# Second attention of a two-layer diffusion backbone: another spread of two projections, and orders between products

## The chip, the cores and the metric

The kernel runs on one core of one Trainium2 chip. The metric is the device time of one execution in microseconds (us). In the profile the engines are called PE (TensorE matmul), PEld (TensorE weight load), DVE (VectorE), ACT (ScalarE), POOL (GpSimd) and SP (SyncE, which issues most of the DMAs here). A name like L465 is a line of the kernel.

## What is computed

The model has two layers over 1024 latent tokens and 256 context tokens with 1024 features. The first layer has a global and a windowed attention side by side. The second layer has a convolution module and a two-dimensional neighbourhood attention side by side; the results of both go through one output projection. The change lies in the second layer's attention. Cut to that, the reference is:

```python
cv, cgl, cg, dq, dk, dv, dg = split_cols(h_lat @ w_in, ODD_WIDTHS)
c_dk, c_dv = heads(x_dk, 8), heads(x_dv, 8)          # context keys and values
oc = conformer_conv(cv, cgl, cg, dw_w, dw_b, ln_g, ln_b)
def d_row(args):                                     # one grid row of 64 queries
    r, qr = args
    rs = clip(r - 4, 0, rows - 8)                    # 8 rows of keys around it
    kk = concat([c_dk, k_grid[rs : rs + 8]])
    vv = concat([c_dv, v_grid[rs : rs + 8]])
    return gqa_attend(qr, kk, vv, bias)              # softmax(q k / 8 + bias) v
od = lax.map(d_row, (arange(rows), q_rows))
y_lat = concat([oc, od * silu(dg)]) @ w_out
return rms_norm(x_lat + g_l * y_lat, final_g)
```

## The kernel before

**Number format.** Each float32 operand of a product is split into a high and a low part. A product is then three matmuls that accumulate into one bank: high by high, high by low, low by high (`mm3`, lines L318, L320, L319). `split` (L296 for the high part, L299 for the low part) makes the two parts. The last matmul of the latest product is kept in `done[0]`.

**Projections of the second attention.** The eight heads are worked in four pairs. `d_proj(i)` projects query, key, value and gate of pair `i`: 31 steps, each a yield after two or three of the eight 128-feature slices `dk`. The order is query chunk 1, query chunk 2, key chunks 1, 2 and 0 (the context), and then, with new weights, value and gate of chunks 1 and 2 and the value of chunk 0. One chunk has 512 tokens, the context 256. A chunk's eight slices are 24 matmuls. The results go to DRAM (`QD`, `KD`, `VD`, `GD`) and are loaded from there. Weights come through `load_w` (L329 loads, eight buffers each for the high and low part, so that the eight slices of one half take all of them). Pairs 0 and 1 are projected beside the convolution and the layer norm. The layer norm (`ln_steps`, L1157 to L1164) uses a memory pool that is closed before the pool of the attention opens; the keys (`KAt`, loaded at L361) are among the tiles that come into that space.

**Attention.** `attn_gen` walks over 16 groups (one head, half of the query columns each) with 7 tiles of keys: 112 tiles. It is a generator: twelve steps of start-up (maxima `mx`, L1342 and L1350, of the first two groups), then two steps a tile. The first step of a tile emits its score product (`st`, L465 and L469), the addition of the bias, the exponential and the split; the second emits the value product (`ov`, L409 to L411) of the tile three before. The first matmul of each score product is appended to the list `sts`, which is shared by both layers.

**Order.** `weave(main, nmain, fill, nfill, ...)` takes `nmain` steps of the attention and spreads `nfill` steps of a projection among them. The fill steps get a priority that is 98 instructions earlier (`FL`), and a planner orders the instructions of each engine by priority and its own estimate of when they are ready. With `lag` above zero a fill step's TensorE instructions are put behind the score product that is `lag` from the end of `sts` (`tc.issue_after`, an order on the engine and no semaphore). Each engine works through its queue in the planned order.

The second attention weaves like this: 73 steps with `d_proj(2)` (31 fill steps), 53 with `d_proj(3)` (31), 77 with the first half of the output projection `out1_part(range(4))` (32), 24 with further parts of it (8), and 12 with its end. The output projection's first half reads the convolution's result (`oc`, loaded and split by `out1_alloc` into buffers that held the normalized tokens).

Of the kernel before, what the change touches and what calls it, by code (L numbers as in the profile page):

```python
# [53 lines left out]
PCB = 3  # L54
MODP = ((), (1, 3, 6))
FL = (80, -98)
LAG = (0, 0, 6, 12)
WV = (73, 53, 77, 24, 12)
SQ = (0, 1)
EV0 = "e0 c0 f0".split()  # L60
EVS = "e1 c1 e2 f1 c2 f2".split()
# [5 lines left out]
ENDS = ((0, 0, 512), (1, 0, 256), (1, 256, 256))  # L67
LATE = 100
NFILL = (34, 34, 34)
HV = (('gggvvvvg',) * 3, ('gggvvvvg', 'vvvgvvvg', 'gggvvvvg'))  # L70
O1 = (6, 84, 46, 14)
TICK0, TICK1 = (1, 3)
# [15 lines left out]
def tile_kernel(ctx: ExitStack, tc: tile.TileContext, a, out):  # L88
    nc = tc.nc
    VE, SC, GP, PE, SY = nc.vector, nc.scalar, nc.gpsimd, nc.tensor, nc.sync  # L90
# [8 lines left out]
    turn = [0, 0]  # L99
    mk, mwp, hold, layer = [0], [None], [0], [0]  # L100
    sts, pvs = [], []

    def bank(tag, name):
        if tag == "pp" and solo[0]:
            turn[0] += 1
            tag = ("pp", "mx")[turn[0] // 2 % 2]
        return ps.tile([P, 512], F32, tag=tag, name=name, bufs=BUFS[tag])
# [3 lines left out]
    def nm(s):  # L111
        uid[0] += 1
        return f"{s}_{uid[0]}"
# [150 lines left out]
    @contextmanager  # L264
    def later(n):

        p = tc.cur_priority
        tc.cur_priority = p + n
        yield
        tc.cur_priority -= n  # L270
# [23 lines left out]
    def split(src, hi, lo, heng="s", leng="g"):  # L294
        if heng == "s":
            SC.copy(hi, src)  # L296
        else:
            VE.tensor_copy(hi, src)
        (GP if leng == "g" else VE).tensor_tensor(lo, src, hi.bitcast(F32), op=ALU.subtract)  # L299

    def make_h(l, c, xs, bc, h):

        cond = 1 if c == 0 else 0
        for dk in range(DK):
            x = xs(dk)
            VE.scalar_tensor_tensor(x, x, gs[l][:, dk, cond : cond + 1], bc, op0=ALU.mult, op1=ALU.mult)
            shift = modT[l][:, dk, cond : cond + 1]
            if HV[l][c][dk] == "v":
                SC.activation(h[0][:, dk, :], x, AF.Identity, bias=shift)
# [2 lines left out]
                SC.activation(x, x, AF.Identity, bias=shift)  # L312
                split(x, h[0][:, dk, :], h[1][:, dk, :])

    done = [None]

    def mm3(o, lh, ll, rh, rl, first, last):
        PE.matmul(o, lh, rh, start=first, stop=False)  # L318
# [73 lines left out]
    def attn_gen(pool, groups, vshare, look, nexts=None):  # L392
# [43 lines left out]
        def prepare(x, n):  # L436

            while n and work and work[0][0] <= x:
                if next(work[0][1], work) is work:
                    work.pop(0)  # L440
                else:
                    n -= 1
# [7 lines left out]
        for x, (g, t) in enumerate(items):  # L450
            if x + AHEAD < len(items):
                items[x + AHEAD][0].ahead(items[x + AHEAD][1])
            if t == 0:
                g.start()
                while any(p is g.prep for _, p in work):
                    prepare(len(items), 1)
                for k in g.ids:
                    next(preps[k])
                    work.append((x + LEAD[layer[0]], preps[k]))
            rate = g.rate * max(len(work), 1)  # L460
            k, q0, n, extra = g.tiles[t]
            KA, KB = g.k()
            st = bank("st", nm("st"))
            cs = slice(k * P, (k + 1) * P)
            sts.append(PE.matmul(st[:, :n], KA[:, cs], g.QH[:, q0 : q0 + n], start=True, stop=False))  # L465
            if not g.bias:
                for lhs, rhs in extra():
                    PE.matmul(st[:, :n], lhs, rhs, start=False, stop=False)
            PE.matmul(st[:, :n], KB[0:68, cs], g.QL[0:68, q0 : q0 + n], start=False, stop=True)  # L469
            ph = pool.tile([P, 512], F32R, tag="ph", name=nm("ph"), bufs=look + 1)  # L470
            pl = pool.tile([P, 512], F32R, tag="pl", name=nm("pl"), bufs=look + 1)
            pf = pool.tile([P, 512], F32, tag="pf" if layer[0] else "ost", name=nm("pf"), bufs=PFB)
            if g.bias and extra is not None:
                VE.tensor_tensor(pf[:, :n], st[:, :n], extra(), op=ALU.add)
                SC.activation(pf[:, :n], pf[:, :n], AF.Exp)
            else:
                SC.activation(pf[:, :n], st[:, :n], AF.Exp, scale=1.0 if g.bias else SCALE)  # L477
            cnt[0] += 1
            split(pf[:, :n], ph[:, :n], pl[:, :n], "s", "v" if cnt[0] % vshare == 0 else "g")
            pend.append((g, t, ph, pl))  # L480
            if t == len(g.tiles) // 2:
                g.gate()
            if t == len(g.tiles) - 1:
                g.last()
            prepare(x, rate // 2)
            yield
            if len(pend) > look:
                flush()
            prepare(x, rate - rate // 2)
            yield  # L490
# [1 line left out]
            flush()  # L492
            yield

    def weave(main, nmain, fill, nfill, last=True, all_fill=True, lag=0):

        done = 0
        for k in range(nmain):
            next(main, None)
            while done * nmain < (k + 1) * nfill:  # L500
                with ExitStack() as cx:
                    cx.enter_context(later(FL[layer[0]]))
                    if lag and len(sts) >= lag:
                        cx.enter_context(tc.issue_after(sts[-lag].ins))
                    next(fill, None)
                done += 1
        if all_fill:
            for _ in fill:
                pass
        if last:  # L510
            for _ in main:
                pass
# [139 lines left out]
    with ExitStack() as p0x:  # L652
# [229 lines left out]
        main = attn_gen(a0, [group0(u, qb) for u in ORDER for qb in QORD], VS0, LOOK0)  # L882
        for k in range(3):
            u = ORDER[k]
            n = NSTEP[u // 2] + (12 if k == 0 else 0)
            n0 = 0 if k else N0
            if not k:
                weave(main, n0, proj_gate(u, gblocks(k)[1]), 9, False)
            weave(main, n - n0 - NLAST[u // 2], fill0(k + 1), NFILL[k], False)
            weave(main, NLAST[u // 2], proj_gate(ORDER[k + 1], gblocks(k + 1)[1]), 18, False)  # L890
# [208 lines left out]
    with ExitStack():  # L1099
# [337 lines left out]
        def out1_part(fs, ks=(0, 1)):  # L1437
            for e2 in range(4):
                w = load_w(wp, a["od_wo"], e2 * 256, 256, 256, WB, dks=fs)
                for e in (2 * e2, 2 * e2 + 1):  # L1440
                    if fs[0] == 0:
                        x2_load(e)
                    for k in ks:
                        yield from out1(fs, e, k, *w)
# [57 lines left out]
                    yield from final_norm(k, bcs[k])  # L1502

        main = attn_gen(dpool, groups1, VSH, LOOK1, {11: [], 12: [13, 14], 13: [15]})
        weave(main, WV[0], d_proj(2), 31, False, True, LAG[0])
        weave(main, WV[1], d_proj(3), 31, False, True, LAG[1])
        run(out1_alloc())
        weave(main, WV[2], out1_part(range(4)), 32, False, True, LAG[2])
        assert fin[0] >= 12
        for hf in (1, 0):  # L1510
            od_load(hf)
        weave(main, WV[3], out1_part((4, 5, 6), (1,)), 8, False, True, LAG[3])
        assert fin[0] >= 14
        weave(main, WV[4], ends(EV0), NEV, False, True)
        wend = [load_w(wp, a["od_wo"], e2 * 256, 256, 256, WB, lambda dk: "gv"[dk % 2], dks=[7]) for e2 in range(4)]
# [118 lines left out]
```

## Time and profile before

| | us |
|---|---|
| median of 3 runs | 1556.66 |
| range of the runs | 1556.37 to 1558.11 |
| profiled execution | 1555.72 |
| span of the profiled execution | 1553.9 |
| TensorE busy in the span | 1449.1 |
| mean granted TensorE clock | 0.967 |

In the tables of the trace by stretches each row has the stretch, its length, and for each engine its busy time and, in brackets, its instructions; then the mean granted TensorE clock (1 is full), the DMA engines' busy share and the GB/s moved. In a timeline a row has start, duration, engine, line, operation, output and inputs, and in square brackets the idle time before it with what ended it. Matmuls are pipelined, so a duration of 0.40 us for a 512-column matmul is longer than the distance to the next.

### The profile page before, as it was taken

What the parts mean: (1) busy time and instruction counts of PE and PEld (TensorE: products, weight loads), DVE (VectorE), ACT (ScalarE), POOL (GpSimd) and SP (SyncE); (2) the same over time, 40 slices, a digit from 0 to 9 for tenths busy, and PEclk for the clock granted to TensorE, in tenths of its full rate; (3) what the DMA queues carried; (4) which work ended last, traced back from release to release, by engine and by line L of the source; (5) the groups of instructions that cost most, each with busy time, mean ns of one, the idle gap of its engine ahead of it and who ended that gap; (6) DMA issues with size and microseconds to landing.
All of it is one profiled execution on the core that took longest, in us unless ns stands there. A gap on an engine that the chain in (4) does not pass through costs nothing.

```text
span 1553.9 us, 22052 instructions
## 1 busy us (share of the span) xinstructions
PE 1449.1 (93%) x6984; PEld 1172.3 (75%) x6984; DVE 1123.3 (72%) x2172; ACT 759.8 (49%) x1545; POOL 833.5 (54%) x762
## 2 busy tenths in 40 slices
PE   6989989999999989899999889999999999799995
PEld 1878868887789678678887668888787787687784
DVE  4998898689858666654577677999755457586776
ACT  2721354445454755565455555443434455545563
POOL 1561464555555676675455666664542443545574
PEclk9999999999999999999999999999999999899996
DMA  9548245423441124631111121213456888788623
GB/s 339 194 146 270 79 125 174 147 64 121 151 129 44 54 89 143 207 115 56 42 45 35 68 95 57 80 63 123 158 178 222 272 225 263 221 264 240 192 92 109
DMA packets 185614, 221.01 MB, mean 142 GB/s; under 512 B 17421, under 2 KB 139481, under 8 KB 185497
## 3 DMA queue, kind: packets, MB, share of 16 engines
q1 hardware_dynamic: 178832, 208.03, 43.1%
q10 hardware_dynamic: 6664, 11.57, 2.3%
q8 instruction: 55, 0.90, 0.2%
q14 instruction: 63, 0.51, 0.1%
HBM read 159.51 MB, written 60.03 MB: 141 GB/s over the span
## 4 chain that ended last, share of the span: by engine, by line
PE 67%; DVE 12%; DMA 11%; issue 3%; POOL 3%; ACT 2%; SPq 2%; DVEq 0%; ACTq 0%; POOLq 0%
PE p L320 6%; PE p L318 6%; PE p L319 6%; PE ov L409 4%; PE ov L410 4%; PE ov L411 4%; PE st L465 4%; PE po L318 4%; PE st L469 4%; PE po L319 4%; PE po L320 4%; PE pq L320 2%; PE pq L319 2%; PE pq L318 2%; DMA mw<-in_mod_w_dram 2%
## 5 line engine op out<-in xcount | busy, mean ns | idle before, releaser
L299 POOL TENSOR_TENSOR pl<-pf,ph 128x512 fp32r<-128x512 f32 (+4 forms) x321 | 399.9, 1258 | 270.7 <-ACT ph L296 218.9
L299 POOL TENSOR_TENSOR wl<-wr,wh 128x256 fp32r<-128x256 f32 (+2 forms) x256 | 197.7, 788 | 227.9 <-ACT wh L296 203.3
L477 ACT ACTIVATE pf<-st 128x512 f32<-128x512 f32 x284 | 166.2, 596 | 161.7 <-PE st L469 106.3
L296 ACT CAST ph<-pf 128x512 fp32r<-128x512 f32 (+4 forms) x364 | 209.2, 588 | 25.5 <-PE ov L410 17.6
L296 ACT CAST wh<-wr 128x256 fp32r<-128x256 f32 (+2 forms) x264 | 103.2, 404 | 172.2 <-DMA wr<-in_od_d_dram 39.3
L318 PE MATMUL p<-hh,wh 128*128 128x512 f32 x448 | 177.7, 399 | 3.7 <-DVE spk L299 1.4
L319 PE MATMUL p<-hl,wh 128*128 128x512 f32 x448 | 177.9, 398 | 0.2 <-POOL hl L299 0.2
L320 PE MATMUL p<-hh,wl 128*128 128x512 f32 x448 | 175.2, 399 | 0.1
L465 PE MATMUL st<-QH,KAt 128*128 128x512 f32 (+4 forms) x364 | 144.0, 397 | 19.8 <-ACT pf L477 16.5
L409 PE MATMUL ov<-ph,Vt 128*128 128x512 f32 (+4 forms) x364 | 143.6, 394 | 8.8 <-DVE y L631 6.4
L411 PE MATMUL ov<-pl,Vt 128*128 128x512 f32 (+4 forms) x364 | 143.7, 395 | 3.9 <-POOL pl L299 3.8
L410 PE MATMUL ov<-ph,Vt 128*64 128x512 f32 (+4 forms) x364 | 140.8, 387 | 0.0
L469 PE MATMUL st<-QL,KBt 68*128 68x512 f32 (+4 forms) x364 | 138.2, 388 | 0.8 <-DVE QL L388 0.7
L1116 DVE SCALAR_TENSOR_TENSOR cps<-U,taps,cps 128x512 f32<-128x512 f32 x184 | 124.3, 747 | 0.0
L589 DVE TENSOR_REDUCE mp<-mx 128x1 f32<-128x512 f32 x128 | 85.5, 682 | 33.5 <-PE mx L588 32.7
L219 DVE SCALAR_TENSOR_TENSOR macc<-mw,csil,macc 128x512 f32<-128x512 f32 x107 | 97.5, 929 | 14.0 <-DMA mw<-in_mod_w_dram 13.2
L318 PEld LDWEIGHTS p<-hh,wh 128*128 128x128 f32 x448 | 84.6, 189 | 24.5 <-DVE spk L299 1.6
L465 PEld LDWEIGHTS st<-QH,KAt 128*128 128x128 f32 x364 | 69.8, 192 | 42.5 <-ACT pf L477 25.3
L319 PEld LDWEIGHTS p<-hl,wh 128*128 128x128 f32 x448 | 84.6, 189 | 20.4 <-POOL hl L299 0.6
L320 PEld LDWEIGHTS p<-hh,wl 128*128 128x128 f32 x448 | 84.6, 189 | 20.3 <-POOL wl L299 1.0
L411 PEld LDWEIGHTS ov<-pl,Vt 128*128 128x128 f32 x364 | 71.1, 195 | 28.1 <-POOL pl L299 7.6
L409 PEld LDWEIGHTS ov<-ph,Vt 128*128 128x128 f32 x364 | 71.5, 196 | 24.3 <-issue 7.0
(277 smaller groups left out, 3518.4 us busy)
## 6 DMA issues: line engine op xcount, KB each, us to landing
mw<-in_mod_w_dram SPq DMA_DIRECT2D x34, 512.0 KB, 5.6
bs<-in_d_bs_dram SPq DMA_DIRECT2D x16, 832.0 KB, 7.3
Q<-qs SPq DMA_DIRECT2D x40, 256.0 KB, 2.7
QH<-Q SPq DMA_DIRECT2D x80, 128.0 KB, 2.7
bm<-in_d_bm_dram SPq DMA_DIRECT2D x16, 540.0 KB, 6.1
wr<-in_od_d_dram SPq DMA_DIRECT2D x64, 128.0 KB, 2.6
mw<-in_mod_w_dram SPq DMA_DIRECT2D x28, 256.0 KB, 3.1
wr<-in_ev_qkv_dram SPq DMA_DIRECT2D x32, 192.0 KB, 3.8
```

Source lines behind the costliest of these rows:

```text
L296: SC.copy(hi, src)
L299: (GP if leng == "g" else VE).tensor_tensor(lo, src, hi.bitcast(F32), op=ALU.subtract)
L318: PE.matmul(o, lh, rh, start=first, stop=False)
L319: PE.matmul(o, lh, rl, start=False, stop=False)
L320: done[0] = PE.matmul(o, ll, rh, start=False, stop=last)
L409: PE.matmul(o, V[:, 64:192], ph[:, :n], start=(t == 0), stop=False)
L410: PE.matmul(g.ov[0:64, q0 : q0 + n], V[:, 0:64], ph[:, :n], start=False, stop=False)
L411: pvs.append(PE.matmul(o, V[:, 64:192], pl[:, :n], start=False, stop=(last and g.sink is None)))
L465: sts.append(PE.matmul(st[:, :n], KA[:, cs], g.QH[:, q0 : q0 + n], start=True, stop=False))
L469: PE.matmul(st[:, :n], KB[0:68, cs], g.QL[0:68, q0 : q0 + n], start=False, stop=True)
L477: SC.activation(pf[:, :n], st[:, :n], AF.Exp, scale=1.0 if g.bias else SCALE)
L1116: VE.scalar_tensor_tensor(pc, uc, w, pc, op0=ALU.mult, op1=ALU.add)
```

## The change

`d_proj(3)` is spread over 73 attention steps instead of 53, and the first half of the output projection over 57 instead of 77 (the sum of the first three weaves stays 203). `LAG` becomes 4 in the first three weaves, where it was 0, 0 and 6. A new number `TIE = 2` puts the score product of an attention step behind the last matmul of the last but one fill step of the same weave. For that, `weave` keeps a list `past` of the last matmul after each fill step, and `attn_gen` reads `tied[0]`. (`prods` is the same list as `done` in the outer function; it has another name because `weave` has a local `done`.)

```diff
-LAG = (0, 0, 6, 12)
-WV = (73, 53, 77, 24, 12)
+LAG = (4, 4, 4, 12)
+WV = (73, 73, 57, 24, 12)
+TIE = 2
...
+    tied = [None]
...
-    done = [None]
+    done = prods = [None]
...
-            sts.append(PE.matmul(st[:, :n], KA[:, cs], g.QH[:, q0 : q0 + n], start=True, stop=False))
+            with ExitStack() as cx:
+                if tied[0] is not None:
+                    cx.enter_context(tc.issue_after(tied[0].ins))
+                sts.append(PE.matmul(st[:, :n], KA[:, cs], g.QH[:, q0 : q0 + n], start=True, stop=False))
...
-    def weave(main, nmain, fill, nfill, last=True, all_fill=True, lag=0):
+    def weave(main, nmain, fill, nfill, last=True, all_fill=True, lag=0, tie=0):
 
         done = 0
+        past = []
         for k in range(nmain):
+            tied[0] = past[-tie] if tie and len(past) >= tie else None
             next(main, None)
+            tied[0] = None
             while done * nmain < (k + 1) * nfill:
                 with ExitStack() as cx:
                     cx.enter_context(later(FL[layer[0]]))
                     if lag and len(sts) >= lag:
                         cx.enter_context(tc.issue_after(sts[-lag].ins))
                     next(fill, None)
+                past.append(prods[0])
                 done += 1
...
-        weave(main, WV[0], d_proj(2), 31, False, True, LAG[0])
-        weave(main, WV[1], d_proj(3), 31, False, True, LAG[1])
+        weave(main, WV[0], d_proj(2), 31, False, True, LAG[0], TIE)
+        weave(main, WV[1], d_proj(3), 31, False, True, LAG[1], TIE)
         run(out1_alloc())
-        weave(main, WV[2], out1_part(range(4)), 32, False, True, LAG[2])
+        weave(main, WV[2], out1_part(range(4)), 32, False, True, LAG[2], TIE)
```

## The prediction

> **What bounds the kernel now.** I read the page first, then the busy time of each engine by stretches of the second attention, then TensorE's timeline at the borders of those stretches, and last what TensorE waited for. The page says that TensorE is the engine to watch:
>
> ```profile
> span 1553.9 us, 22052 instructions
> PE 1449.1 (93%) x6984; PEld 1172.3 (75%) x6984; DVE 1123.3 (72%) x2172; ACT 759.8 (49%) x1545; POOL 833.5 (54%) x762
> ```
>
> The span is 1553.9 us. Inside the part that the change touches I cut at events: the first product of the third head pair (1172.7), its 63rd (1189.2), the first key load landed (1212.7), the last product of the fourth pair (1334.5), the first output product (1361.6), a key wait (1446.6), the last scores (1518).
>
> ```profile
> core 0: us, PE busy (x) PEld busy (x) DVE busy (x) ACT busy (x) POOL busy (x), PEclk, DMA share, GB/s
> 1172.70:1189.20 16.50, 16.47 (x80) 13.63 (x81) 10.34 (x22) 6.12 (x14) 5.00 (x6) 1.00 0.70 224
> 1189.20:1212.70 23.50, 20.19 (x97) 16.09 (x95) 6.99 (x14) 7.60 (x16) 9.27 (x12) 1.00 0.74 223
> 1212.70:1230.40 17.70, 17.10 (x81) 13.50 (x82) 9.10 (x24) 5.21 (x10) 0.00 (x0) 1.00 1.06 327
> 1230.40:1334.50 104.10, 99.11 (x516) 81.75 (x515) 70.87 (x170) 57.35 (x128) 46.03 (x51) 0.98 0.79 239
> 1334.50:1361.60 27.10, 19.59 (x78) 14.66 (x79) 14.10 (x35) 14.84 (x31) 12.76 (x14) 0.75 0.89 232
> 1361.60:1446.60 85.00, 80.39 (x393) 65.07 (x391) 63.31 (x155) 44.60 (x91) 42.18 (x44) 1.00 0.88 251
> 1446.60:1518.00 71.40, 70.94 (x337) 57.97 (x338) 50.94 (x106) 45.38 (x100) 50.00 (x52) 0.98 0.40 122
> ```
>
> Stretch minus PE busy is idle: 0.0 + 3.3 + 0.6 + 5.0 + 7.5 + 4.6 + 0.5 = 21.5 us. One minus PEclk, times the stretch, is what the slower clock took: 2.1 (fourth pair's stretch) + 6.8 (27.1 x 0.25) + 1.4 = 10.3 us. No product is added or removed, so the change can only move this loss of 31.8 us. Its worst part is 1334.5 to 1361.6: 7.5 + 6.8 = 14.3 us in which attention runs without a projection beside it.
>
> Why that hole is there:
>
> ```profile
> 1315.63 1.89 DVE L299 TENSOR_TENSOR oc<-oc 128x512 fp32r<-128x512 f32 x3
> 1337.42 1.67 POOL L299 TENSOR_TENSOR wl<-wr,wh 128x256 fp32r<-128x256 f32 x2
> 1361.22 0.50 PE L465 MATMUL st<-QH,KAt 128*128 128x512 f32 x1
> 1361.78 0.40 PE L318 MATMUL po<-oc,wh 128*128 128x512 f32 x1
> ```
>
> The inputs of the output projection were split by 1317.5 and its first weights by about 1339, yet its first product comes at 1361.78, right behind a score product. The score count by stretch says which one:
>
> ```profile
> core 0: us, PE busy (x) PEld busy (x), PEclk, DMA share, GB/s
> 1212.70:1230.40 17.70, 0.51 (x2) 0.42 (x3) 1.00 1.06 327
> 1230.40:1334.50 104.10, 13.22 (x39) 7.30 (x39) 0.98 0.79 239
> 1334.50:1361.60 27.10, 5.26 (x12) 2.78 (x12) 0.75 0.89 232
> 1361.60:1446.60 85.00, 12.39 (x36) 6.59 (x35) 1.00 0.88 251
> ```
>
> 2 + 39 + 12 = 53 scores. In program order twelve start-up steps come first and then every second step emits a score, so after 73 + 53 steps and the first of the third weave 58 scores exist; the sixth from the end is the 53rd. So LAG[2]=6 held the output projection back, while the unbound projections (LAG 0, priority 98 earlier) had run out at score 41.
>
> **The change part by part.**
>
> *(a) The hole.* The fourth pair's 31 fill steps now spread over 73 attention steps, and steps and scores keep within a window. Its last products come near the 62nd score instead of near the 41st, and the first output product after the 65th. Three scores lie between, and at the 85 / 36 = 2.4 us a score of the next stretch they give 7 us for the weight splits. I take 1 us left of the 14.3; bounds 0 and 7.5.
>
> *(b) The start.* LAG[0] goes from 0 to 4. `sts` still holds the first layer's scores, so the bound is free until four new scores stand in the list, which is after step 18 (scores at steps 12, 14, 16, 18). Fill step j is emitted after step floor(73j/31): j = 7 after 16, j = 8 after 18. So steps 0 to 7 are free, and from step 8 on the products stand behind the first score of this attention. Eight steps are query chunk 1 (24 products), query chunk 2 (24) and the key chunk's first five of eight (15): 63 products, or 21 of each line. How far they reach, and what is behind them now:
>
> ```profile
> 1172.70:1189.20 16.50, 8.51 (x21) 3.95 (x21) 1.00 0.70 224
> 1189.20:1212.70 23.50, 12.00 (x33) 6.00 (x32) 1.00 0.74 223
> 1189.33 0.40 PE L320 MATMUL p<-hh,wl 128*128 128x512 f32 x1
> 1189.80 0.39 PE L319 MATMUL p<-hl,wh 128*128 128x512 f32 x1
> 1203.03 0.69 DVE L1163 SCALAR_TENSOR_TENSOR uc<-uc,gc 128x512 f32<-128x512 f32 x1 [3.15 <-DMA gc<-Gc]
> 1203.75 0.33 SPq L1164 DMA_DIRECT2D Oc<-uc  x1
> 1206.60 1.14 SPq L361 DMA_DIRECT2D KAt<-KD  x2
> 1212.74 0.47 PE L1342 MATMUL mx<-KAt,QH 128*128 128x256 f32 x2 [1.95 <-DMA KAt<-KD]
> 1213.25 0.51 PE L465 MATMUL st<-QH,KAt 128*128 128x512 f32 x2
> ```
>
> ```profile
> gc<-Gc SPq DMA_DIRECT2D x3, 256.0 KB, 3.4
> Q<-qs SPq DMA_DIRECT2D x40, 256.0 KB, 2.7
> ```
>
> (The first two rows count L318 alone; the last two are DMA issues with their size and us to landing, near the start and on the page.) The 21st triple ends at 1189.2. The first score cannot move up much: it needs the first keys, and their load goes out only when the layer norm's buffers are free, 2.8 us after the last `Oc` store is issued; that store ends a chain of `gc` loads through one buffer. The projection's key stores and weight loads now leave that chain some DMA time; I give it 1.5 us, so the first score comes at 1211.2 and TensorE idles 1211.2 - 1189.2 = 22 us where 3.3 were idle. Bounds: 18 (three `gc` loads 0.7 us shorter each, 2.7 against 3.4, and a key load shortened by as much in all) and 25. The 20.2 us of products done there now come later.
>
> *(c) The ramp.* Only fill steps 8 and 9 (15 products, 3.5 us at the 0.47 / 2 of the rows above) stand free behind scores 1 and 2; step 10 needs score 3, which needs a score bank, and so the first exponential, and so the maxima of the first group:
>
> ```profile
> 1213.26 0.69 DVE L1344 TENSOR_REDUCE mp<-mx 128x2 f32<-128x512 f32 x1 [9.54 <-PE mx L1342]
> 1218.51 0.15 DVE L377 TENSOR_REDUCE nmt<-mp 128x4 fp32r<-128x8 f32 x1
> ```
>
> That is 5.4 us on VectorE, about 8 us with transpose, mask and exponential (an estimate), against 6 to 7 us of TensorE work at full clock. The clock will not be full: after the weaker stall at 1334.5 the clock took 6.8 us. I charge 4 us for clock and idle together; bounds 0 and 8. [...]
>
> *(d) The bound stretch.* Until the projections end TensorE has 139 of 160 triples left at 3 x 0.235 = 0.70 us, 32 of them (context chunk) at half, so 86 us; and 67 scores. A score's whole attention work is 1.07 us: in 1361.6 to 1446.6 PE is busy 80.39 us, of which 180 products
>
> ```profile
> L318 PE MATMUL po<-oc,wh 128*128 128x512 f32 x60 | 24.0, 400 | 0.0
> ```
>
> (60 of each line, 42 us by spacing) leave 38.4 us for 36 scores. 86 + 72 = 158 us, 2.4 us a score. The stretch just named ran bound too (LAG 6, at its limit from the first product on), at 2.4 us a score, and lost 4.6 / 80.4 = 6%; the unbound one lost 5.0 / 99.1 = 5%. I take 5%: 8 us, with 2.1 us of clock. Bounds 2 and 18; the upper one holds if the second binding decides, below.
>
> *(e) The output projection over 57 steps.* Same products for 28 scores instead of 38, so 2.6 us a score: more cover. Loss 4 us (bounds 2 and 8), of which this row's wait returns, since head 7 is loaded at a fixed group:
>
> ```profile
> 1446.65 0.50 PE L1342 MATMUL mx<-KAt,QH 128*128 128x256 f32 x2 [2.77 <-DMA KAt<-KD]
> ```
>
> After step 203 nothing changes: 0.5 + 1.4 us. ACT, DVE and POOL get the same instructions; none is a bound by the first table.
>
> Sum of the loss after: 22 + 4 + 8 + 2.1 + 1 + 4 + 1.9 = 43, against 31.8: 11 us longer, rounded to **10** because (d) and (e) use the upper of their nearest rows. The profiled execution took 1555.72 us with 1.8 us around the span; it is 0.9 below the median 1556.66. So span 1564, median 1566.5.
>
> **The rivals.**
>
> *A. The bindings remove more than the start costs (faster).* Mechanism: with work always beside it, attention never stands alone, so the hole goes and steady losses fall to 2%. 18 + 0 + 3 + 1 + 0 + 2 + 1.9 = 26 us, 6 less than 31.8: 1551. It wins where the start idles under about 20 us and (d) loses under 4. For it: the hole is 14.3 us, and 1446.6 to 1518 idles 0.5 in 71. Against it: it needs low ends throughout, while DMA is at a share of 0.79 to 0.89 and waits for keys are DMA waits.
>
> *B. The score binding becomes a wait (clearly slower).* TIE=2 stops a score until the last but one fill step is done. Where new weights come in, fill stands:
>
> ```profile
> 1234.27 0.70 ACT L296 CAST wh<-wr 128x256 fp32r<-128x256 f32 x2
> 1249.83 0.41 ACT L296 CAST wh<-wr 128x256 fp32r<-128x256 f32 x1 [1.02 <-DMA wr<-in_od_d_dram]
> ```
>
> Eight weights take 16 us, where three bound fill steps take about 8.5. Now scores run on freely; bound, they stop after two fill steps, some 2.4 scores, and behind the waiting score on TensorE stand the maxima, the value products and every later fill step. Three such changes (third pair's second half, both halves of the fourth) at 4 to 5 us add 13 us, 8 of them beyond my 5%, and a clock loss of half the 6.8 us above for the idle: some 4 us. 1566.5 + 8 + 4 = 1579. Against it: fill may enter the change four scores ahead.
>
> *C. The losses balance (no difference).* 18 + 2 + 5 + 1 + 3 + 1.9 = 31 us in the order (b), (c), (d), (a), (e), rest: 1556 to 1557.
>
> *D. The early binding does not act*, because the planner finds other products for the gap: then (b) is 3.3 and (c) nothing, 20 us in all: 1545. The program order above speaks against it.
>
> **How the numbers follow.** Forecast (1560 to 1573) 0.50; B 0.18; C 0.12; A 0.16; D 0.04. A measurement of this kernel can tell about 0.2%, 3.1 us. Faster 0.20, within 0.12, slower 0.68. The range leaves out D and the ends of A and B: 1551 to 1583. The forecast's own range is 1560 to 1573.
>
> **What would show it.** Right: about 20 us of TensorE idle ending at the first `mx` that waits for `KAt`, 21 triples of the third pair ahead of it; no stretch of attention without `p` or `po` between the fourth pair's end and the first `po`, which follows the 65th score; PEclk near 1 there and below 1 behind the start. Wrong: products of L318 between 1190 and the first L465; or PE idle at `st` in front of each weight change by more than 3 us (then B); or the bound stretch losing under 3% (then A).

## The result, and the profile after

The changed kernel takes 1580.81 us (median of 4 runs, 1577.3 to 1585.7), the kernel before 1556.51 us beside it (1555.31 to 1558.11). The ratio is 1.0158 with a 95% interval of 1.0125 to 1.019, so the change makes the kernel about 24 us slower. 1566.5 us was forecast, with a range of 1551 to 1583: the direction was right and the range holds the result, but the forecast's own range of 1560 to 1573 does not, and the step of 10 us came out at 20 to 24 (the smaller number is from a second measurement of the same program, below). The profiled execution of the changed kernel took 1578.39 us. Lines moved down by the change: L318 to L320 are now L320 to L322, L465 is L470, L1342 is L1351, L1350 is L1359. The head of the page:

```profile
span 1576.5 us, 22033 instructions
PE 1454.4 (92%) x6984; PEld 1177.2 (75%) x6984; DVE 1125.1 (71%) x2172; ACT 762.3 (48%) x1545; POOL 833.6 (53%) x762
```

TensorE has the same 6984 instructions and is busy 5 us more in a span that is 22.6 us longer. So the time is idle time, and the lower clock behind it (0.83 granted in the 30.1 us behind the new gap). The stretches of the changed kernel, cut at the same kind of events as before: first product of the third pair, last product ahead of the gap, first score, end of the clock's ramp, last product of the fourth pair, first output product, a key wait, end of the last value product.

```profile
core 0: us, PE busy (x) PEld busy (x) DVE busy (x) ACT busy (x) POOL busy (x), PEclk, DMA share, GB/s
1176.20:1190.90 14.70, 14.70 (x72) 12.03 (x72) 8.39 (x18) 5.84 (x12) 5.02 (x6) 1.00 0.76 249
1190.90:1213.90 23.00, 0.18 (x1) 0.01 (x1) 6.86 (x13) 2.80 (x3) 3.58 (x4) 0.55 0.48 133
1213.90:1244.00 30.10, 28.49 (x126) 23.07 (x127) 17.87 (x47) 12.79 (x27) 9.08 (x10) 0.83 0.78 251
1244.00:1398.20 154.20, 141.74 (x717) 116.04 (x716) 95.25 (x234) 80.78 (x169) 60.26 (x66) 0.98 0.78 224
1398.20:1400.40 2.20, 2.20 (x15) 1.87 (x15) 0.48 (x1) 1.79 (x5) 2.15 (x4) 1.00 0.74 211
1400.40:1477.00 76.60, 75.57 (x369) 62.06 (x367) 51.44 (x125) 38.17 (x82) 41.39 (x45) 1.00 0.91 264
1477.00:1541.50 64.50, 62.47 (x288) 49.99 (x286) 46.78 (x87) 40.44 (x89) 45.54 (x48) 0.97 0.35 100
1541.50:1576.50 35.00, 17.73 (x91) 15.88 (x90) 25.18 (x60) 9.99 (x26) 17.04 (x17) 0.65 0.34 121
```

Read as in the prediction, idle is the stretch minus PE busy, and the clock's loss is the stretch times one minus PEclk. The hole of the kernel before (27 us with 14.3 lost) is gone: 2.2 us, nothing lost. In its place stand a gap of 22.8 us ahead of the first score, a ramp behind it (1.6 idle + 5.1 clock), and a bound stretch up to 1398.2 (bound: each product stands behind a score in TensorE's order) that loses 12.5 + 3.1. The rest loses 1.0, and 2.0 + 1.9. Together that is 50.0 us where the kernel before lost 31.8. The rows at the borders, from TensorE's timeline:

```profile
1190.68 0.40 PE L322 MATMUL p<-hh,wl 128*128 128x512 f32 x1
1213.93 0.77 PE L1351 MATMUL mx<-KAt,QH 128*128 128x256 f32 x2 [22.85 <-DMA KAt<-KD]
1379.30 0.39 PE L413 MATMUL ov<-pl,Vt 128*128 128x512 f32 x1
1385.05 0.76 PE L1351 MATMUL mx<-KAt,QH 128*128 128x256 f32 x2 [5.37 <-DMA QH<-QD]
1385.98 0.49 PE L470 MATMUL st<-QH,KAt 128*128 128x352 f32 x1
1386.27 0.63 PE L320 MATMUL p<-hh,wh 128*128 128x512 f32 x1
1400.42 0.40 PE L320 MATMUL po<-oc,wh 128*128 128x512 f32 x1
```

The gap ends at the first maxima, which waits for its keys, as forecast. The later rows show how the bound stretch loses: at 1385.05 the maxima of a new group waits 5.37 us for its queries; a score stands behind it in TensorE's order, and only behind that come projections. What TensorE waited for in that stretch (us, times, longest):

```profile
engine line waited for: us in total, times, longest us
PE mx L1351 <- DMA QH<-QD: 8.8, 4, 5.4
PE ov L411 <- DVE y L1376: 1.7, 1, 1.7
```

8.8 of its 12.5 us of idle time are four such waits for `QH`. Behind each of the four stands a score, and behind that a projection.

### The profile page after: what moved, and what is told of

Same layout as the page of the kernel before. It is cut to its first block, busy times and chain, and to the rows that moved or that the text cites. A ratio compares the mean times of both kernels' runs of the same rounds, so it can differ in the third digit from the quotient of the medians.

```text
span 1576.5 us, 22033 instructions
## 1 busy us (share of the span) xinstructions
PE 1454.4 (92%) x6984; PEld 1177.2 (75%) x6984; DVE 1125.1 (71%) x2172; ACT 762.3 (48%) x1545; POOL 833.6 (53%) x762
## 4 chain that ended last, share of the span: by engine, by line
PE 67%; DVE 13%; DMA 12%; issue 3%; POOL 2%; ACT 1%; SPq 1%; DVEq 0%; POOLq 0%; ACTq 0%
PE p L322 6%; PE p L320 6%; PE p L321 6%; PE po L320 4%; PE po L321 4%; PE ov L411 4%; PE po L322 4%; PE ov L413 4%; PE ov L412 4%; PE st L470 4%; PE st L474 4%; DMA mw<-in_mod_w_dram 3%; PE pq L322 2%; PE pq L321 2%; PE pq L320 2%
## 5 line engine op out<-in xcount | busy, mean ns | idle before, releaser
L298 ACT CAST ph<-pf 128x512 fp32r<-128x512 f32 (+4 forms) x364 | 209.6, 588 | 21.0 <-PE ov L412 13.4
L320 PE MATMUL p<-hh,wh 128*128 128x512 f32 x448 | 178.6, 400 | 1.7 <-DVE spv L301 0.8
L322 PE MATMUL p<-hh,wl 128*128 128x512 f32 x448 | 176.4, 400 | 0.4 <-POOL wl L301 0.2
L470 PE MATMUL st<-QH,KAt 128*128 128x512 f32 (+4 forms) x364 | 144.4, 398 | 13.0 <-ACT pf L482 12.7
L413 PE MATMUL ov<-pl,Vt 128*128 128x512 f32 (+4 forms) x364 | 143.3, 394 | 4.0 <-DVE pl L301 2.4
L598 DVE TENSOR_REDUCE mp<-mx 128x1 f32<-128x512 f32 x128 | 85.6, 683 | 34.9 <-PE mx L597 33.9
L320 PEld LDWEIGHTS p<-hh,wh 128*128 128x128 f32 x448 | 85.3, 190 | 22.1 <-ACT wh L298 1.7
L322 PEld LDWEIGHTS p<-hh,wl 128*128 128x128 f32 x448 | 85.0, 190 | 21.3 <-POOL wl L301 1.2
L470 PEld LDWEIGHTS st<-QH,KAt 128*128 128x128 f32 x364 | 70.0, 193 | 33.4 <-ACT pf L482 20.3
```

The lines of the kernel that those rows point to most:

```text
L322: done[0] = PE.matmul(o, ll, rh, start=False, stop=last)
L413: pvs.append(PE.matmul(o, V[:, 64:192], pl[:, :n], start=False, stop=(last and g.sink is None)))
```

## The experiments

The theory at first was that of the prediction: the start's gap is the price, and the rest is bought and sold at about the same value. Its rivals were the score binding, the bound stretch with its query waits, and the spreading. Each kernel was timed beside the kernel before on the same chip, and ratios are to that. The losses in the table are worked out like those above, from three stretches of each kernel's one profiled execution: first product of the third pair to the first maxima, from there to the end of the last value product, and the tail behind it. PEclk has two digits, so the clock behind the first score is uncertain by about 1.6 us; after and e2 turn out to be one program, and their rows show how far two executions differ.

| kernel | ratio, 95% interval | idle ahead of first score | behind it: idle + clock | tail | all three stretches |
|---|---|---|---|---|---|
| before | 1 | 3.3 | 18.5 + 9.3 | 32.8 | 381.2 |
| after | 1.0158, 1.0125 to 1.019 | 22.8 | 17.1 + 9.8 | 34.9 | 400.3 |
| e1_lag0_free | 1.0109, 1.0087 to 1.0131 | 3.2 | 27.0 + 19.6 | 33.0 | 399.6 |
| e2_no_tie | 1.0127, 1.0109 to 1.0145 | 22.8 | 16.7 + 13.2 | 34.9 | 401.6 |
| e3_hole_only | 1.0106, 1.0085 to 1.0128 | 3.5 | 22.0 + 15.8 | 39.4 | 395.8 |
| e4_start_only | 1.0163, 1.0142 to 1.0183 | 22.5 | 15.8 + 9.8 | 38.2 | 400.9 |
| e5_lead5 | 1.0108, 1.008 to 1.0136 | 23.0 | 16.6 + 9.9 | 33.4 | 400.7 |
| e6_lag_20_14 | 1.0046, 1.0027 to 1.0065 | 3.5 | 19.2 + 12.6 | 34.9 | 389.6 |
| e7_before_lead5 | 1.0007, 0.9989 to 1.0024 | 3.5 | 18.1 + 9.3 | 32.4 | 381.0 |
| e8_spread_only | 1.009, 1.006 to 1.012 | 3.3 | 22.3 + 26.0 | 35.3 | 400.1 |
| e9_taper20 | 1.0038, 1.0018 to 1.0059 | 3.6 | 19.1 + 12.4 | 37.5 | 387.5 |
| e10_taper12 | 1.0054, 1.003 to 1.0078 | 14.7 | 12.4 + 9.3 | 38.2 | 389.6 |
| e11_before_taper | 0.9984, 0.9963 to 1.0006 | 3.6 | 17.9 + 9.2 | 31.5 | 378.0 |
| e12_start4 | 1.002, 0.9996 to 1.0044 | 19.9 | 11.5 + 6.3 | 35.6 | 386.9 |

The first product of the third pair, ahead of everything that these kernels change, came between 1170.9 and 1179.8 us in the 14 executions (1176.2 in after, 1173.9 in the same program of e2). That is why the last column leaves out what lies ahead of it.

### First set: the two bindings, the score binding, the hole

**e1_lag0_free**, the start's binding taken back in the changed kernel:

```diff
-LAG = (4, 4, 4, 12)
+LAG = (0, 4, 4, 12)
```

> The changed kernel with LAG[0] back at 0: only the third pair's projection is unbound again. Theory S (the start's binding is the cost): TensorE's idle ahead of the first keys falls from 22.8 us to 3 to 5, the half clock behind it (5.1 us) and the ramp's 1.6 us go, so about 25 us less than the changed kernel: 1553 to 1558. Rival G (the two other bindings and the new spread cost as well, the stretch up to the projections' end losing 12.5 us whatever the start is): 1562 to 1568 though the start is repaired.

Measured: 1575.33 us. Both theories missed. The gap at the start closed (3.2 us idle for 22.8), and as much reappeared later (46.6 us behind the first score for 26.9). Three stretches of this kernel:

```profile
1215.10:1244.00 28.90, 28.06 (x142) 22.78 (x143) 18.73 (x50) 12.94 (x29) 7.79 (x10) 0.94 0.89 287
1244.00:1285.00 41.00, 29.73 (x109) 22.11 (x108) 23.22 (x60) 19.72 (x39) 17.39 (x18) 0.75 0.73 210
1285.00:1395.00 110.00, 100.61 (x488) 81.92 (x489) 69.65 (x165) 57.13 (x115) 37.98 (x40) 0.94 0.70 208
```

The third pair's projections were used up early, and the fourth pair's could not begin before their own lag of 4: attention ran alone from 1244 to 1285, without one projection, with 11.3 us idle and 10.3 of clock (41 x 0.25). That is a hole like that of the kernel before, at another place and longer.

**e2_no_tie**, the score binding taken away:

```diff
-TIE = 2
+TIE = 0
```

> The changed kernel with TIE = 0: no score product is bound to a fill product. Theory S: the score binding never acts, since fill has priority and is always ahead of the place it is asked for: 1577 to 1585, the changed kernel's time, and the same 22 to 23 us of idle at the start. Rival B (the score binding is a wait at the changes of weights): 8 to 13 us less than the changed kernel, 1568 to 1573.

Measured: 1577.67 us, an interval that overlaps that of the changed kernel. The program is the same, instruction for instruction, with and without `TIE`: the products that a score is bound to already stand ahead of it. So the score binding does nothing here, theory S's expectation held, and rival B of the prediction can't be the cause. So these are two measurements of one program, and together the better measure of the change: the three stretches take 19.1 and 20.4 us more than before.

**e3_hole_only**, the kernel before with only the hole's lag widened:

```diff
-LAG = (0, 0, 6, 12)
+LAG = (0, 0, 16, 12)
```

> The kernel before with LAG[2] = 16 in place of 6, nothing else: the first output product may come after the 43rd score instead of the 53rd. Theory H (LAG[2] made the hole, and its 14.3 us are real loss): the stretch without a projection shrinks from 27 us to under 6, and the time falls by 8 to 12 us to 1545 to 1549. Rival M (the hole only moves, since the output products then run out ten scores earlier in the following stretch): within 3 us of the kernel before, 1553 to 1560.

Measured: 1574.94 us. Both theories missed again. The first row below is what is left of the hole, the second a stretch that begins where the output products ran out:

```profile
1343.90:1351.80 7.90, 6.61 (x27) 4.84 (x27) 5.83 (x15) 4.80 (x13) 4.76 (x7) 0.78 0.86 278
1447.00:1483.00 36.00, 28.49 (x114) 21.17 (x115) 24.62 (x61) 18.30 (x36) 18.35 (x19) 0.82 0.65 180
```

The hole fell to 7.9 us, and one of 36 us opened (7.5 idle, 6.5 clock); the tail grew by 6.6 us as well.

**e4_start_only**, the kernel before with only the start bound:

```diff
-LAG = (0, 0, 6, 12)
+LAG = (4, 0, 6, 12)
```

> The kernel before with LAG[0] = 4, nothing else: only the start is bound. Theory S: 20 to 23 us of idle and 5 us of clock at the start; the third pair's products pushed out of it then lie beside later scores, which shortens the hole (14.3 us) by part: 1566 to 1578. Rival N (the planner fills the gap, or the products pushed out close the whole hole and the two cancel): 1553 to 1562.

Measured: 1584.36 us, above the expected 1566 to 1578.

```profile
1192.60:1215.00 22.40, 0.00 (x0) 0.00 (x0) 6.49 (x12) 2.81 (x3) 3.58 (x4) 0.61 0.47 138
1244.00:1375.10 131.10, 127.03 (x663) 105.48 (x662) 82.84 (x195) 69.91 (x151) 53.28 (x59) 1.00 0.79 237
1375.10:1540.40 165.30, 155.16 (x728) 123.26 (x725) 111.82 (x252) 90.65 (x194) 95.47 (x101) 0.98 0.64 187
```

The gap is there, and the stretch up to the output products is good (4.1 idle in 131), with the products held back now in it. But the output stretch loses 10.1 + 3.3 and the tail 5.4 more than before. At this point I took the start's gap for the whole price; e12 below has nearly the same gap and pays far less.

### Second set: the query waits, the spreading, a wider lag

**e5_lead5** and its control **e7_before_lead5**: loads of a group written one score tile earlier, in the changed kernel and in the kernel before.

```diff
-LEAD = (3, 4)
+LEAD = (3, 5)
```

> The changed kernel with LEAD = (3, 5): the preparation of a group (its key and query loads, its biases) is written one score tile earlier. Theory Q: the part of the bound stretch that the prediction sized too small (12.5 us idle where 8 were expected) is the wait of scores for the query tile QH (8.8 us in 4 waits, 5.37 us the longest), because a bound product may not come early and fill that wait. With a tile more of lead, about 2.4 us, each of the four waits loses up to 2.4 us, so 4 to 8 us go: 1571 to 1576 us, and the QH row of the waits falls under 4 us. Rival, place: the transfers are bound by their queue and not by when they are written, or other waits (banks, vectors) take their place: 1576 to 1582 us, with the idle time of the bound stretch still near 12 us. The start idle of about 22 us stays in both.

> The kernel before with LEAD = (3, 5), the control of the changed kernel with that lead. Its waits for QH are 1.3 us in 2. Theory Q: there is nothing to gain, 1555 to 1558 us. Rival, place: whatever the earlier preparation is worth, it is worth it in both kernels, so the time moves as in the changed kernel with that lead, up or down by the same amount within 3 us.

Measured: 1576.06 and 1560.66 us. The waits for queries in the bound stretch of e5:

```profile
PE mx L1351 <- DMA QH<-QD: 6.3, 4, 2.2
PE ov L411 <- DVE y L1376: 2.1, 2, 1.7
```

They fell from 8.8 to 6.3 us and not under 4, and the idle time behind the first score from 17.1 to 16.6. All three stretches take 400.7 us, no less than the 400.3 of the changed kernel. The ratio's interval overlaps with that of e2. So a gain from the earlier loads isn't shown. But the run hardly tests theory Q, since the edit hardly moved the loads. At the four places that wait in the changed kernel, the time from the issue of the query load to its first maxima is 8.0, 8.7, 8.8 and 10.9 us there and 8.0, 8.1, 8.4 and 9.2 in e5, and the TensorE work in it 7.0, 7.9, 7.1 and 5.5 us against 7.1, 5.8, 7.2 and 7.2. Only the last place got more work ahead of it, and its wait fell from 5.4 to 2.0 us. What loads that really start earlier would be worth stays open. In the kernel before no gain shows, as expected.

**e8_spread_only**, the spreading without the bindings:

```diff
-WV = (73, 53, 77, 24, 12)
+WV = (73, 73, 57, 24, 12)
```

> The kernel before with WV = (73, 73, 57, 24, 12) and its own LAG = (0, 0, 6, 12): the spreading half of the change without the binding half. The projections still run ahead freely, so the start stays covered (idle under 5 us ahead of the first score) and the projections end at the same score as before, about the 41st, while the output products come 20 scores later in the program and are held by lag 6 until about the 64th score. Theory stock: the stretch without products, 27 to 29 us long in the kernel before, grows to about 45 to 55 us, and its loss (idle and slow clock, 13 to 15 us of the 31.8) grows in proportion by 8 to 14 us: 1564 to 1571 us. Rival, border: the loss at such a stretch is a fixed price of its two borders and not of its length, so the time stays at 1555 to 1560 us. If it comes out at the time of the changed kernel (1576 to 1582 us), the spreading explains the loss without any binding.

Measured: 1574.91 us, 4 us above theory stock's range; the ratio times 1556.5, from which that range was worked out, is 1570.5 and inside it. The stretch of attention alone, from the 40th to the 64th score:

```profile
1340.30:1391.90 51.60, 39.82 (x141) 28.37 (x141) 33.12 (x85) 26.77 (x54) 21.98 (x24) 0.73 0.80 221
```

51.6 us long with 11.8 idle and 13.9 of clock, 25.7 us where the kernel before lost 14.3 in 27.1 us. Length and loss both fit theory stock: the loss grows with the length (about half a microsecond per microsecond alone, in these two). Note that spreading and start binding cost 0.9% and 1.6% alone, and 1.3 to 1.6% together with the other bindings: they aren't additive. It fits that the binding keeps back the products that the spread stretch lacks.

**e6_lag_20_14**, everything bound, but with a wide lag that is given back in steps:

```diff
-LAG = (4, 4, 4, 12)
+LAG = (20, 17, 14, 12)
```

> The changed kernel with LAG = (20, 17, 14, 12): a fill step may start once the score 20, 17, 14 or 12 places ahead of it has been issued, instead of 4, 4, 4, 12. So the first 20-odd steps of the third pair's projection are free and can run while the start waits for the keys, and the lead that they gain is given back in small steps instead of at one place. Theory lead: the loss of the change is the start alone, which needs products that may run ahead of the scores; with free products the idle time ahead of the first score falls from 22.8 us to under 5, no stretch of scores alone appears longer than 8 us, and the time is below the kernel before: 1545 to 1556 us. Rival, stock: the products that run in the start are missing later; the lag of the second weave then holds the fill for about as long as the start took, spread over the borders of the weaves, with idle time and a slow clock there: 1560 to 1572 us.

Measured: 1567.51 us at a ratio of 1.0046, about 7 us above the kernel before and in theory stock's range. Start and long hole are both mended, and it still isn't faster. One stretch stands out:

```profile
1446.00:1476.00 30.00, 23.86 (x84) 16.64 (x85) 21.30 (x54) 13.21 (x26) 14.55 (x15) 0.76 0.62 180
```

The output products, 14 scores early now, had run out at 1446 as in e3: 6.1 idle and 7.2 clock.

### Third set: an even lag, and the price of the gap by itself

Three kernels use a lag that may change from step to step:

```diff
-                    if lag and len(sts) >= lag:
-                        cx.enter_context(tc.issue_after(sts[-lag].ins))
+                    if lag:
+                        n = lag[0] + (lag[1] - lag[0]) * done // nfill if isinstance(lag, tuple) else lag
+                        if len(sts) >= n:
+                            cx.enter_context(tc.issue_after(sts[-n].ins))
```

**e9_taper20**: the changed kernel with `LAG = ((20, 20), (20, 13), (13, 6), 12)`.

> The changed kernel with a lag that falls evenly from step to step: 20 for the third pair's projection, 20 to 13 over the fourth's, 13 to 6 over the first output products, 12 behind. Some 20 steps are free for the start, and from there the steps stand about evenly, 0.7 to 0.95 to a score, up to the 89th score. Theory lead: the price is set by the places where the lag between products and scores is taken up at once. The start idle falls to about 3 us, no stretch of scores without products is longer than 5 us, and what the kernel with lags 20, 17, 14, 12 lost at 1436 to 1476 (7.2 us idle and 6.8 us of clock, where its output products had run out) goes too: 1542 to 1553 us, below the kernel before. Rival, density: a score with one product step beside it is no faster than the alternation of the kernel before, since queries, banks and vectors then wait instead; then it stays at 1556 to 1568 us, with idle time and clock behind the first score of 25 us or more.

Measured: 1562.49 us, ratio 1.0038: the rival, density. Its first stretch behind the start, and the place where e6 had run out:

```profile
1213.40:1360.90 147.50, 136.21 (x676) 111.19 (x677) 98.11 (x238) 79.40 (x165) 56.92 (x62) 0.95 0.82 247
1448.00:1473.00 25.00, 21.74 (x94) 17.67 (x93) 19.70 (x46) 11.58 (x26) 16.31 (x17) 0.86 0.61 186
```

The long stretches without products are gone (the second row loses 3.3 + 3.5), yet the first loses 11.3 + 7.4, in waits of at most 2.4 us each. Theory density's reason, too few products beside each score once 36.6 us of TensorE work are spent ahead of the first, fits this and isn't tested by itself.

**e10_taper12**: the same with `LAG = ((12, 12), (12, 9), (9, 6), 12)`.

> The same even lag from 12 instead of 20: 12, then 12 to 9, then 9 to 6, 12 behind. About 12 steps are free for the start. Theory lead: the start idle stands between the 22.8 us of lag 4 and the 3.4 us of lag 20, since 8 more steps of about 1.7 us are free than with lag 4: about 9 us idle (7 to 13) ahead of the first score, and the time is 8 to 14 us above the same kernel with 20 free steps and 12 to 18 below the changed kernel: 1555 to 1567 us. Rival, threshold: the price is a fixed one for any gap ahead of the first score (the clock falls and has to come back), so the time is that of the changed kernel, 1574 to 1581 us.

Measured: 1563.59 us. The gap and the bound stretch:

```profile
1202.70:1217.40 14.70, 0.05 (x1) 0.03 (x1) 2.12 (x4) 3.87 (x7) 7.22 (x10) 0.66 0.80 239
1240.00:1378.20 138.20, 133.79 (x687) 109.39 (x686) 90.90 (x221) 75.35 (x160) 56.71 (x61) 0.99 0.76 230
```

The time lies in theory lead's range, but its working doesn't hold: the gap is 14.7 us and not 7 to 13, and this kernel is 1.1 us above e9 where 8 to 14 were expected. Eleven microseconds more of gap cost next to nothing: the loss behind the first score is 21.7 us against 31.5. The threshold theory falls too.

**e11_before_taper**: the kernel before with `LAG = (0, (20, 6), 6, 12)`, which draws out the fourth pair's projections into the hole.

> The kernel before, with its own numbers of steps (73, 53, 77, 24, 12), where only the lag of the fourth pair's projection is changed: it falls from 20 to 6 over that projection instead of none. The start stays free as before; the projections of the fourth pair are drawn out to about the 53rd score, where the output products begin, so the stretch of scores alone (40th to 53rd score, 29.3 us, 8.6 us idle and 6.7 us of clock) has products again. Theory lead: 9 to 15 us of its 15.3 go: 1541 to 1549 us. Rival, density: what is taken from the first 40 scores makes those as much slower, and the time stays within 4 us of the kernel before.

Measured: 1554.51 us, ratio 0.9984 with an interval that holds 1: no gain that can be told, as density has it. The hole is gone and its loss stands in front of it:

```profile
1218.80:1363.20 144.40, 134.28 (x675) 110.16 (x676) 93.63 (x233) 77.92 (x163) 56.14 (x61) 0.95 0.83 246
1363.20:1525.00 161.80, 154.07 (x745) 124.56 (x743) 112.40 (x258) 91.60 (x193) 95.16 (x102) 0.99 0.66 194
```

**e12_start4**: the gap of the changed kernel with a looser lag behind it, `LAG = ((4, 12), (12, 9), (9, 6), 12)`.

> The changed kernel with a lag that grows from 4 to 12 over the third pair's projection, and then goes as in the kernel with the even lag from 12: 12 to 9, 9 to 6, 12. The start is bound as in the changed kernel (about 72 products and 22 us idle ahead of the first score); only the lag behind it is looser. Theory tight lag: what the changed kernel loses behind the start besides the ramp of the clock (15.5 us up to the end of the projections) comes from the lag of 4, by which a product can't be taken into a wait of the scores; with 12 that stretch loses 5 to 8 us, as the 5.8 idle and 6.4 clock of the even lag from 12: 1564 to 1572 us, 7 to 15 below the changed kernel. Theory start: the gap of 22 us with its slow clock is the whole price, so the time is that of the changed kernel, 1575 to 1581 us, whatever the lag behind it. Theory stock: products not spent in the start are worth their time later wherever the lag lets them in, so the gap itself costs nearly nothing (the kernel with 14.65 us idle at the start is only 1.1 us above the one with 3.6): 1558 to 1564 us.

Measured: 1563.09 us, ratio 1.002 (0.9996 to 1.0044). The gap, the ramp, the bound stretch and the rest:

```profile
1192.80:1212.70 19.90, 0.01 (x1) 0.00 (x1) 3.85 (x7) 1.69 (x2) 3.58 (x4) 0.62 0.67 198
1212.70:1235.00 22.30, 20.63 (x80) 16.59 (x81) 12.20 (x34) 8.51 (x17) 7.23 (x9) 0.73 0.90 268
1235.00:1373.00 138.00, 137.16 (x723) 114.68 (x722) 94.68 (x225) 76.65 (x166) 59.16 (x63) 1.00 0.78 235
1373.00:1525.70 152.70, 143.76 (x692) 115.97 (x690) 107.18 (x235) 86.09 (x186) 92.06 (x98) 1.00 0.67 195
```

And what TensorE waited for from 1244 to the end of the projections:

```profile
PE trv L1237 <- DVE sgd L1229: 0.6, 1, 0.6
PE p L320 <- ACT wh L298: 0.2, 1, 0.2
```

The gap of 19.9 us and its ramp are there, and yet the kernel is only 0.2% above the kernel before, with an interval that holds 1. Behind the ramp TensorE idles 0.8 us in 138 at full clock, where the changed kernel idles 12.5 in 154. The row ends just ahead of a wait, though, and part of the gain returns behind it, where e12 idles 8.9 us in 152.7 and the changed kernel 3.1 in 143.3 (L1353 here is L1351 of the changed kernel):

```profile
1375.29 0.48 PE L1353 MATMUL mx<-KAt,QH 128*128 128x256 f32 x2 [1.86 <-DMA QH<-QD]
```

Theory start falls. Of the other two the time fits theory stock's range (1558 to 1564) and is 1 us below tight lag's; by the ratio (1559.6 on 1556.5) it is 4 us below. After's interval (1.0125 to 1.019, or 1.0109 to 1.0145 for e2) and this one don't touch, so the lags behind the start decide the greater part of the loss: in the last column 13.4 (400.3 minus 386.9) of 19.1 us. By the table 2.9 of the 13.4 lie in the gap, and 9.1 in the idle time and the clock behind it.

Do the products stand ahead of the waits now, as theory tight lag has it? The rows run from the issue of a query load to the first maxima that reads it, for the four groups that wait in the changed kernel (first four rows) and for the same groups in e12:

```profile
1256.53:1264.50 7.97, 7.01 (x39) 5.51 (x38) 1.28 (x3) 4.98 (x10) 2.79 (x3) 1.00 1.02 295
1298.56:1307.25 8.69, 7.93 (x39) 6.24 (x37) 1.76 (x5) 4.94 (x9) 3.33 (x3) 1.00 1.01 257
1336.24:1345.05 8.81, 7.07 (x46) 5.95 (x44) 3.12 (x8) 5.17 (x10) 4.37 (x5) 1.00 1.01 277
1374.16:1385.05 10.89, 5.53 (x28) 4.23 (x28) 4.57 (x12) 5.74 (x12) 2.32 (x2) 0.98 1.03 266
1256.40:1265.07 8.67, 8.67 (x44) 7.10 (x43) 3.75 (x10) 5.66 (x11) 2.46 (x3) 1.00 1.00 268
1289.97:1300.92 10.95, 10.95 (x53) 8.89 (x52) 5.71 (x16) 6.71 (x13) 4.64 (x5) 1.00 0.98 287
1326.76:1336.84 10.08, 10.08 (x51) 8.28 (x49) 4.21 (x13) 5.12 (x10) 4.48 (x5) 1.00 1.02 278
1367.53:1375.29 7.76, 5.32 (x37) 4.58 (x37) 5.10 (x14) 5.84 (x13) 4.33 (x5) 1.00 1.01 280
```

For the first three they do: the loads take as long to land in both (at most 7.4, 8.2 and 8.3 us against 7.2, 8.4 and 8.0), but TensorE has 8.7 to 11.0 us of work ahead of the maxima instead of 7.0 to 7.9. These three waits are 3.5 of the 8.8 us. The fourth and longest is another matter: 5.3 us of work stand ahead of it in e12, no more than the 5.5 of the changed kernel, but the load lands after 7.0 us instead of 10.2. In the 10 us ahead of its issue the DMA engines were busy at a share of 0.97 in the changed kernel (1364 to 1374, `oc` loads among it) and 0.44 in e12 (1357.5 to 1367.5). A load that queues behind others fits that wait; no run tests it.

## Why the prediction was right, and where it was off

**(a) The hole**: held. 1 us was left in the sum, 0 measured; the first output product came behind the 65th score as forecast. But e1, e3 and e11 show no way to win the 14.3 us in it: in each of them the hole is gone or short, and its loss stands elsewhere.

**(b) The start**: held, 22.8 us for 22. Two errors partly cancel, which is luck: 18 triples stood ahead of it instead of 21 (the row x72 holds 54 products and 18 others), so the work ended 1.8 us sooner, and the keys came 37.7 us after the third pair's first product where 38.5 were expected.

**(c) The ramp**: 6.7 us for 4, inside its bounds of 0 to 8.

**(d) The bound stretch**: this is the term that was mis-sized, 15.6 us (12.5 idle + 3.1 clock) for 10.1 (8 + 2.1). It was priced by the 5 to 6% idle of its nearest rows, an unbound stretch and one with lag 6. The measured share of idle is 12.5 / 141.7 = 9%. A rate taken from rows with another lag did not hold: 8.8 us are waits for queries, in front of products that were bound behind them. In the kernel before TensorE waited for query loads 0.8 us from 1215 to 1400, so no row there could have given that size; the term's upper bound of 18 did hold it.

**(e) and the rest**: 1.0 + 3.9 for 4 + 1.9. The wait for keys of 2.77 us came back as 1.0.

**The sum**: 50.0 us of loss for 43, against 31.8, so 18 instead of 11. The forecast's 11 was rounded down to 10 with the reason that (d) and (e) stood at their upper rows; for (d) that was wrong, since it took 5%, the lower of its two rows. The tail, which the sum held fixed, is 2.1 us longer. In the single profiled execution 3.5 more lie ahead of the first changed instruction; e2, the same program, has 1.2 of them, so they are not shown to be the change's.

**The attribution** was only half right. The gap at the start was forecast as the place where the change loses, and it is the largest new loss in the trace. Yet the gap alone does not set the price: e12 keeps 19.9 us of it and pays 0.2%, e4 keeps 22.5 us and pays 1.6%. The prediction moved 20.2 us of products out of the gap and then gave the stretches that received them the loss rates of the kernel before, as if those products could not fill later waits. In e12 they do in part, with 17.8 us lost behind the first score against 27.8 in the kernel before; with the lag of 4 of the changed kernel they don't (26.9). So the sum got the sign and half of the size for this kernel by a rule that does not hold in general: the same sum for e12 would have come out some 7 us too high (10 forecast, 0.2% or 3 us measured).

**The rivals**: B's time, 1579, was met and its mechanism is refuted by e2. The stated range reaches to 1583 on B's account, so that it holds the result is in part luck. A, C and D ended elsewhere; the gap of 22.8 us speaks against D directly.

**What stays open**: e12 differs from the changed kernel in three lags, so which of them does most isn't settled. Whether the busier DMA queue ahead of the fourth query load (issued 1374.16, and 1367.53 in e12) made its longer way, and whether that comes from the lag, was not tested. Nor is it settled why e4, with the same gap and a free second weave, loses 25.6 us behind it and e12 17.8, or why the tails differ by up to 8 us.

## What to carry to other kernels

Filler work is a fixed stock: before a gap or a hole is charged at its length, ask where the work that is missing there will run instead, and whether the order lets it stand in front of a wait. A filler bound close behind the work it is meant to cover leaves less of itself ahead of that work's waits (here 7.0 to 7.9 us at three query waits, against 8.7 to 11.0 with the looser lag), and what stands behind a wait in the engine's order did not fill it (the maxima at 1385.05 waited 5.37 us, and the projection behind it started at 1386.27). Here a lag of 4 scores cost 1.1 to 1.4% against one that opens to 12, and a binding that never acts (`TIE`) cost nothing. Before a run counts against a theory, look in its trace whether the edit moved what it was meant to move: that of e5 hardly did. A loss rate taken from neighbouring stretches belongs to the lag under which they ran.

## What was not expected of the hardware

The clock dipped twice after one gap. Stretches of the changed kernel, in the gap's later part and behind it:

```profile
1197.00:1213.90 16.90, 0.00 (x0) 0.01 (x1) 2.08 (x3) 1.47 (x1) 3.58 (x4) 0.50 0.55 150
1213.90:1217.00 3.10, 3.07 (x9) 2.58 (x10) 1.28 (x3) 0.00 (x0) 0.00 (x0) 0.50 1.03 417
1217.00:1220.00 3.00, 3.00 (x14) 2.50 (x13) 0.56 (x2) 0.85 (x2) 0.00 (x0) 0.96 1.04 415
1220.00:1224.00 4.00, 2.77 (x10) 1.26 (x8) 3.95 (x13) 1.28 (x1) 0.00 (x0) 1.00 1.04 209
1224.00:1228.00 4.00, 3.64 (x11) 2.96 (x12) 3.85 (x12) 1.76 (x5) 0.30 (x1) 0.51 1.16 325
1228.00:1232.00 4.00, 4.00 (x13) 3.15 (x12) 0.57 (x3) 0.38 (x1) 1.67 (x2) 0.64 0.74 294
```

The granted clock is 0.50 at the end of the gap and for 3.1 us of work behind it (1.6 us lost), then 0.96 to 1.00; after a stretch of 4 us in which TensorE was busy for 2.77 it falls to 0.51 again, and 1.96 + 1.44 us are lost there. So two thirds of the ramp's 5.1 us of clock came from a second dip, behind pauses of 1.23 us in all; whether these bring it on was not tested. Behind the gaps of e10 and e12 it stands too: a stretch of 4 us with TensorE busy for 2.83 and 2.89, and then 4 us at 0.50 and 0.74.
